# Token shift, masks, norm rows and value heads in other and wider operations, in a decoder layer of three mixers

## The chip, the cores and the metric

The kernel runs on one core of a Trainium2 chip. The metric is the device time of one execution in microseconds (us); less is better. A core has engines that each work through their own list of instructions in order: PE (TensorE, matrix multiplications; PEld is its loading of weights), DVE (VectorE), ACT (ScalarE), POOL (GpSimd) and SP (which here issues the DMA transfers). They wait for each other by semaphores.

## The reference, cut to what matters

One decoder layer for 512 tokens of width 1024: a norm, one input projection, three mixers side by side (NSA attention, RWKV-7, MoBA attention), an output projection, a ConvGLU and a last norm, all in float32. The change touches RWKV-7's input and its gating matrices, and NSA's values:

```python
def _rwkv7_mixer(p, mu, w0, w2, a0, a2, g2, k_k, k_a, r_k, lnx_w, lnx_b):
    p_prev = jnp.pad(p, ((0, 0), (1, 0), (0, 0)))[:, :-1]
    p = p + (p_prev - p) * mu                       # token shift
    r, k, v, xw, xa, xg = _split(p, [D_RWKV] * 3 + [32, 32, 64])
    w = jnp.exp(-RW_DECAY_SCALE * jax.nn.sigmoid((w0 + jnp.tanh(xw) @ w2).astype(f32)))
    a = jax.nn.sigmoid(a0 + xa @ a2)
    kk = heads(k * k_k)
    kk = kk / jnp.maximum(jnp.sqrt(jnp.sum(kk * kk, axis=-1, keepdims=True)), 1e-12)
    ...
def step(state, inp):                               # scanned over the 512 tokens
    r_t, w_t, k_t, v_t, kk_t, a_t = inp
    sa = jnp.einsum('bhvk,bhk->bhv', state, -kk_t)
    state = state * w_t[:, :, None, :] + sa[..., None] * (kk_t * a_t)[:, :, None, :] + v_t[..., None] * k_t[:, :, None, :]
    return state, jnp.einsum('bhvk,bhk->bhv', state, r_t)
```

NSA multiplies its probabilities with two pairs of value heads of 64 columns (`vs`, `vw`), which are columns of the input projection times the token's norm factor.

## The kernel before, in words

Features stand on the 128 partitions and tokens along the free axis, 512 at a time. A float32 product is made of three matmuls on operands split in a high and a low part (`mm3`, L238 to L243; `whi`, `wlo`, `xh`, `xl` are such parts); the high part is an ACT cast, the low part a DVE subtraction (L211, L213).

First four projections run side by side: the inputs of the decay and gate matrices (LORA) and `r`, `k`, `v` of the first RWKV head pair. After them `merge()` (L1030) interleaves generators: a stream of the other projections in the order of a list (`ks r1 v1 k1 nv q0 ...`), the two RWKV head pairs (`rw_run`, which calls `rw_pair`), and the attentions as their inputs come. Each `yield` carries a cost, and the generator with the least sum goes on. A scheduler of the framework then sets each engine's final list from that program order and its own estimate of when operands are ready, and gives each matmul result one of eight PSUM banks. So an edit that alters a few operations can reorder others and give banks to other results. From about 360 us on only the ConvGLU runs.

The parts that the change touches:

- `rw_in` (L319 to L337), once per RWKV input tile, seven tiles in all (four at the end of the first projections, then `r`, `v`, `k` of the second pair): `ex` is the projection times the norm factor (L325), `d` the difference of neighbour tokens (L330, and L331 for the first token), `rwin` = `d`·mu + `ex` (L335). The first tile is then put through tanh and sigmoid by ACT (L1062, L1063).
- `rw_pair` (L341), once per head pair: three matmuls on the LORA tile (L349, L353, L360); `ksq`, the square of `k`, by ACT (L374); its sums per head by PE (L379); a maximum by DVE (L383); a power by POOL (L386); `rnb`, four broadcast copies by DVE, each followed by a matmul that turns it (L394, L395); and `kkn`, the normalised key, which reads that PSUM bank (L398). Then products of chunks of 64 tokens (L450), masked into `GA` and `GR` (L456).
- The masks `NM` (L467) and `R` (L480), four operations of 128x128 each; `NM` reduced to `Nc` (L474) goes through DRAM to `NB` (L476, L478). A chain of 30 dependent DVE operations inverts 16x16 blocks (`X`, L488 to L490), a copy ends it (L492), and the result goes through DRAM again (L497, L499) to `DvT` and `Dv` (L502).
- `proj_v` (L717): per token tile 24 matmuls of 274 columns, then gates by ACT (L739), and for each of four heads an ACT operation for the high part (L742) and a DVE operation for the low part (L743).
- `evac_q` (L688), for a query tile: `P` (L690) takes it from PSUM, `qt` are its split parts (L695 by ACT, L696 by DVE), and `soft` (L769) starts with the matmul that reads `qt` (L779).

Of the kernel before, what the change touches and what calls it, by code (L numbers as in the profile page):

```python
# [36 lines left out]
F32 = mybir.dt.float32  # L37
F32R = mybir.dt.float32r
# [54 lines left out]
def hybrid_layer(ctx: ExitStack, tc: tile.TileContext, xT, cst, cols, lora, fgain, wA, wVn, cw1,  # L93
# [7 lines left out]
    def at(site):  # L101
        return pool if ENG[site] == 'p' else dve
# [21 lines left out]
    def r2(name, shape=(128, 512), dt=F32):  # L124
        return sb.tile(list(shape), dt, name=name, bufs=cap(name))
# [76 lines left out]
    omka = fixe(2)  # L202
    rcol = fixe(4)
# [108 lines left out]
    def consts_late():  # L312
        sp.dma_start(cstt, cst)
        sp.dma_start(lorat, lora)
        pool.tensor_copy(ident, ident0)
        dve.tensor_scalar(omka, colt[:, COLS["k_a"][0]:COLS["k_a"][0] + 2], -1.0, 1.0, op0=OP.mult, op1=OP.add)


    def rw_in(todo):  # L319

        mark('rwin')
        exs, ds, os_ = [], [], []
        for i, p in todo:
            ex = r2("ex")
            dve.tensor_tensor(ex, p, rstd_box[0], op=OP.mult)  # L325
            done()
            exs.append(ex)
        for ex in exs:
            d = r2("d")
            at('d').tensor_tensor(d[:, 1:512], ex[:, 0:511], ex[:, 1:512], op=OP.subtract)  # L330
            at('d').tensor_scalar(d[:, 0:1], ex[:, 0:1], -1.0, None, op0=OP.mult)  # L331
            ds.append(d)
        for (i, p), ex, d in zip(todo, exs, ds):
            o = r2("rwin")
            dve.scalar_tensor_tensor(o, d, col("mu", i), ex, op0=OP.mult, op1=OP.add)  # L335
            os_.append(o)
        return os_  # L337
# [3 lines left out]
    def rw_pair(p, r, k, v, L):  # L341
# [93 lines left out]
        bsel2 = bs_[:, None, :, None].to_broadcast([128, 2, 4, 16])  # L435
# [43 lines left out]
        for cc in range(4):  # L479
            dve.tensor_tensor(TS(R)[:, cc], GA[cc // 2][:, cc % 2, :, 0, :], con("offmask")[:, None, :].to_broadcast([128, 2, CH]), op=OP.mult)  # L480
# [236 lines left out]
    def proj_v():  # L717
# [835 lines left out]
```

## Time and profile before

| | |
|---|---|
| time, three runs | 729.62, 730.01, 731.35 us (median 730.01) |
| time of the profiled execution | 732.95 us |
| its span, first to last instruction | 731.1 us (so 1.85 us lie around it) |
| mean granted TensorE clock | 0.987 |
| busy | PE 701.1 us (96%), PEld 611.9, DVE 635.6 (87%), ACT 412.5 (56%), POOL 56.4 |

The profile is one execution recorded on the chip. A busy time counts the stretches in which an engine had an instruction under way; a wait is idle time before an instruction, put down to what released it. DVE's rows overlap a little: an instruction of 0.68 us starts 0.60 us after the one before it. The granted clock is a share of TensorE's full 2.4 GHz; 0.52 is about its lower level of 1.2 GHz.

### The profile page before, as it was taken

What the parts mean: (1) busy time and instruction counts of PE and PEld (TensorE: products, weight loads), DVE (VectorE), ACT (ScalarE), POOL (GpSimd) and SP (SyncE); (2) the same over time, 40 slices, a digit from 0 to 9 for tenths busy, and PEclk for the clock granted to TensorE, in tenths of its full rate; (3) what the DMA queues carried; (4) which work ended last, traced back from release to release, by engine and by line L of the source; (5) the groups of instructions that cost most, each with busy time, mean ns of one, the idle gap of its engine ahead of it and who ended that gap; (6) DMA issues with size and microseconds to landing.
All of it is one profiled execution on the core that took longest, in us unless ns stands there. A gap on an engine that the chain in (4) does not pass through costs nothing.

```text
span 731.1 us, 13614 instructions
## 1 busy us (share of the span) xinstructions
PE 701.1 (96%) x5146; PEld 611.9 (84%) x5146; DVE 635.6 (87%) x1394; ACT 412.5 (56%) x863; POOL 56.4 (8%) x71
## 2 busy tenths in 40 slices
PE   6999998899999999999989999999999999999995
PEld 4866977677788788877779999999999999998885
DVE  6589889768897999787999999999999999999804
ACT  7364544465656877863767546455464545657503
POOL 3110003000000010123320000000000000000001
PEclk9999999999999999999999999999999999999998
DMA  9613122513110013033308432323233333345003
GB/s 321 199 29 102 52 48 63 145 52 110 45 44 30 14 45 102 1 101 117 101 0 280 152 103 99 118 87 101 94 110 96 107 102 108 95 130 186 17 1 115
DMA packets 44658, 69.87 MB, mean 96 GB/s; under 512 B 10544, under 2 KB 12208, under 8 KB 44592
## 3 DMA queue, kind: packets, MB, share of 16 engines
q1 hardware_dynamic: 44016, 67.96, 29.4%
q8 instruction: 40, 0.66, 0.4%
q10 hardware_dynamic: 576, 1.05, 0.4%
q14 instruction: 26, 0.21, 0.1%
HBM read 64.40 MB, written 4.59 MB: 94 GB/s over the span
## 4 chain that ended last, share of the span: by engine, by line
PE 75%; DVE 13%; issue 4%; ACT 2%; DMA 2%; POOL 2%; SPq 0%; POOLq 0%; DVEq 0%; ACTq 0%
PE mm L241 6%; PE mm L243 6%; PE mm L242 6%; PE acc L242 5%; PE acc L241 5%; PE acc L243 5%; PE pB L241 3%; PE pB L243 3%; PE pC L241 3%; PE pB L242 3%; PE pC L242 3%; PE pC L243 3%; PE pA L241 3%; PE pA L243 3%; PE pA L242 3%
## 5 line engine op out<-in xcount | busy, mean ns | idle before, releaser
L1302 ACT CAST ah<-S 128x512 fp32r<-128x512 f32 x88 | 54.5, 621 | 60.8 <-DVE S L1297 60.6
L241 PE MATMUL mm<-xh,whi 128*128 128x512 f32 x152 | 68.3, 450 | 1.2 <-DVE Sall L622 1.2
L242 PE MATMUL acc<-dn,dn 128*128 128x512 f32 (+1 forms) x173 | 64.2, 371 | 0.0
L243 PE MATMUL acc<-dn,dn 128*128 128x512 f32 (+1 forms) x173 | 63.7, 370 | 0.0
L243 PE MATMUL mm<-xh,wlo 128*128 128x512 f32 x152 | 61.4, 404 | 0.0
L242 PE MATMUL mm<-xl,whi 128*128 128x512 f32 x152 | 61.1, 402 | 0.0
L1303 DVE TENSOR_TENSOR al<-S,ah 128x512 fp32r<-128x512 f32 x88 | 58.5, 682 | 0.8 <-ACT ah L1302 0.8
L211 ACT CAST whi<-wraw 128x512 fp32r<-128x512 f32 x70 | 42.4, 617 | 26.7 <-PE mm L242 11.9
L786 ACT ACTIVATE prob<-prob,fixed 128x128 f32<-128x128 f32 (+1 forms) x72 | 40.5, 564 | 26.9 <-DVE fixed L783 26.6
L241 PE MATMUL acc<-dn,dn 128*128 128x512 f32 (+1 forms) x173 | 55.7, 371 | 0.0
L241 PE MATMUL pB<-bh,ah 128*128 128x256 f32 x172 | 49.8, 290 | 0.0
L213 DVE TENSOR_TENSOR wlo<-wraw,whi 128x512 fp32r<-128x512 f32 x64 | 46.6, 734 | 2.9 <-PE mm L243 2.8
L241 PE MATMUL pC<-bh,ah 128*128 128x256 f32 x172 | 48.5, 282 | 0.2 <-ACT ah L1302 0.2
L243 PE MATMUL pB<-bh,al 128*128 128x256 f32 x172 | 48.6, 282 | 0.0
L243 PE MATMUL pC<-bh,al 128*128 128x256 f32 x172 | 48.5, 282 | 0.0
L242 PE MATMUL pC<-bl,ah 128*128 128x256 f32 x172 | 48.4, 281 | 0.0
L242 PE MATMUL pB<-bl,ah 128*128 128x256 f32 x172 | 48.3, 281 | 0.0
L1303 DVE TENSOR_TENSOR al<-wraw,ah 128x512 fp32r<-128x512 f32 x66 | 43.4, 681 | 0.0
L783 DVE CUSTOM_DVE_ANT_0 prob<-s,early 128x128 f32<-128x128 f32 (+1 forms) x72 | 34.6, 483 | 7.1 <-PE s L780 4.9
L818 ACT CAST ph<-pt 128x512 fp32r<-128x512 f32 (+3 forms) x72 | 29.4, 423 | 19.1 <-PE pt L811 18.3
L1302 ACT CAST ah<-wraw 128x512 fp32r<-128x512 f32 x66 | 36.7, 616 | 0.6 <-DMA wraw<-in_wF_dram 0.6
L242 PEld LDWEIGHTS acc<-dn,dn 128*128 128x128 f32 x173 | 32.7, 189 | 5.1 <-DVE dn L1366 0.2
(396 smaller groups left out, 2241.2 us busy)
## 6 DMA issues: line engine op xcount, KB each, us to landing
wraw<-in_wF_dram SPq DMA_DIRECT2D x88, 256.0 KB, 2.7
wraw<-in_wG_dram SPq DMA_DIRECT2D x44, 256.0 KB, 2.9
wraw<-in_wA_dram SPq DMA_DIRECT2D x38, 256.0 KB, 2.9
xr<-in_xT_dram SPq DMA_DIRECT2D x16, 256.0 KB, 4.9
wraw<-in_cw_dram SPq DMA_DIRECT2D x16, 256.0 KB, 3.2
wraw<-in_wO_dram SPq DMA_DIRECT2D x16, 256.0 KB, 2.6
fraw<-in_wA_dram SPq DMA_DIRECT2D x8, 256.0 KB, 5.6
x2d<-x2o SPq DMA_DIRECT2D x8, 256.0 KB, 3.7
```

Source lines behind the costliest of these rows:

```text
L211: act.copy(hi[:, :w], raw)
L213: (dve if dve_lo and (wcnt[0] % PLO or wcnt[0] < PLO0) else pool).tensor_tensor(lo[:, :w], raw, hi[:, :w].bitcast(F32), op=OP.subtract)
L241: pe.matmul(o, ah, bh, start=first, stop=False)
L242: pe.matmul(o, ah, bl, start=False, stop=False)
L243: pe.matmul(o, al, bh, start=False, stop=last)
L783: dve.tensor_tensor_reduce(out=P, in0=s_[:, 0:n], in1=con("cmask")[:, 512 - n:512], scale=1.0, scalar=3e38, op0=OP.add, op1=OP.min, accum_ ...
L786: act.activation(P, P, AF.Exp, bias=m, scale=-1.0, accum_out=sums[:, i, par:par + 1])
L818: act.copy(h, t_[:, 0:n])
L1302: act.copy(h, src)
L1303: at(f'L{i}').tensor_tensor(l, src, h.bitcast(F32), op=OP.subtract)
```

## The change

Token shift: `d` is gone. ACT writes `rwin` = `ex`·(1 − mu), and one DVE operation adds mu times the token before to columns 1 to 511. The column 1 − mu (`omu`) is made once. `rnb`: one copy of 128x512 for four of 128x128. `NM` and `R`: two operations of 128x256 each for four of 128x128. Value heads: one ACT and one DVE operation of 4x64 columns per token tile for four of each; they go into one tile `vn` for all heads, where there was a tile `vv` per head. A buffer less for `vv`. Beside that only two tables of sizes and the line of `omu` differ:

```diff
 
     def rw_in(todo):
 
         mark('rwin')
-        exs, ds, os_ = [], [], []
+        exs, os_ = [], []
         for i, p in todo:
             ex = r2("ex")
             dve.tensor_tensor(ex, p, rstd_box[0], op=OP.mult)
             done()
             exs.append(ex)
-        for ex in exs:
-            d = r2("d")
-            at('d').tensor_tensor(d[:, 1:512], ex[:, 0:511], ex[:, 1:512], op=OP.subtract)
-            at('d').tensor_scalar(d[:, 0:1], ex[:, 0:1], -1.0, None, op0=OP.mult)
-            ds.append(d)
-        for (i, p), ex, d in zip(todo, exs, ds):
+        for (i, p), ex in zip(todo, exs):
             o = r2("rwin")
-            dve.scalar_tensor_tensor(o, d, col("mu", i), ex, op0=OP.mult, op1=OP.add)
+            act.activation(o, ex, AF.Identity, scale=omu[:, i:i + 1])
             os_.append(o)
+        for (i, p), ex, o in zip(todo, exs, os_):
+            dve.scalar_tensor_tensor(o[:, 1:512], ex[:, 0:511], col("mu", i), o[:, 1:512], op0=OP.mult, op1=OP.add)
         return os_
 
     lock = [0]
@@ -389,9 +388,9 @@
         yield from want()
         prn = rbank()
         rb4 = r2("rnb", (128, 4, 2, 64))
+        dve.tensor_copy(rb4.rearrange("p a b c -> p (a b) c"), b3(rn2, 64))
         for t in range(NT):
             rb = rb4[:, t]
-            dve.tensor_copy(rb, b3(rn2[:, 2 * t:2 * t + 2], 64))
             pe.matmul(prn[:, t * 128:(t + 1) * 128], rb.rearrange("p a b -> p (a b)"), ident, start=True, stop=True)
         yield crw
         kkn = r2("kkn")
@@ -432,7 +431,6 @@
 
         R64 = ((0, 64), (64, 128))
         bs_ = con("bsel")
-        bsel2 = bs_[:, None, :, None].to_broadcast([128, 2, 4, 16])
         bsel4 = bs_[:, None, :, None].to_broadcast([128, 4, 4, 16])
         TS = lambda t: t.rearrange("p (c h x) -> p c h x", c=4, h=2)
 
@@ -463,9 +461,9 @@
         yield crw
         R, NM = r2("R"), r2("NM")
         NMv = NM.rearrange("p (c b j) -> p c b j", b=4, j=16)
-        for cc in range(4):
-            at('NM').tensor_tensor(NMv[:, 2 * cc:2 * cc + 2], GA[cc // 2][:, cc % 2, :, 0, :].rearrange("p h (b j) -> p h b j", b=4),
-                               bsel2, op=OP.mult)
+        for u in range(2):
+            at('NM').tensor_tensor(NMv[:, 4 * u:4 * u + 4], GA[u][:, :, :, 0, :].rearrange("p k h (b j) -> p (k h) b j", b=4),
+                               bsel4, op=OP.mult)
 
         XT, BT, st_, NX = (r2(n_) for n_ in ("X", "NB", "stmp", "Nc"))
         v16 = lambda z, u: z[0:64, u * 256:u * 256 + 256].rearrange("p (i j) -> p i j", j=16)
@@ -476,8 +474,9 @@
         sp.dma_start(s1.rearrange("c p j -> p c j"), Nc)
         NB = v16(BT, 0)
         sp.dma_start(NB, s1.rearrange("c (b i) j -> (c b) i j", b=8))
-        for cc in range(4):
-            dve.tensor_tensor(TS(R)[:, cc], GA[cc // 2][:, cc % 2, :, 0, :], con("offmask")[:, None, :].to_broadcast([128, 2, CH]), op=OP.mult)
+        for u in range(2):
+            dve.tensor_tensor(ch(R)[:, 4 * u:4 * u + 4], GA[u][:, :, :, 0, :].rearrange("p k h t -> p (k h) t"),
+                              con("offmask")[:, None, :].to_broadcast([128, 4, CH]), op=OP.mult)
         yield crw
         X = v16(XT, 0)
         pool.memset(X, 0.0)
@@ -727,7 +726,7 @@
                 (at('vwl') if i else dve).tensor_tensor(lo, r_, hi.bitcast(F32), op=OP.subtract)
                 wt.append((hi, lo))
             yield CW
-        vv = [q2("vv", (128, NT, 2, 64), F32R) for _ in range(4)]
+        vv = q2("vn", (128, NT, 4, 2, 64), F32R)
         for t in range(NT):
             yield from want()
             p = bank("mm")
@@ -737,13 +736,12 @@
                 if k % 2:
                     yield CW
             act.activation(gates[:, t, :], p[:, 256:274], AF.Sigmoid, scale=rcol[:, t:t + 1])
-            for h in range(4):
-                src = p[:, h * 64:(h + 1) * 64]
-                act.activation(vv[h][:, t, 0, :], src, AF.Identity, scale=rcol[:, t:t + 1])
-                dve.scalar_tensor_tensor(vv[h][:, t, 1, :], src, rcol[:, t:t + 1], vv[h][:, t, 0, :].bitcast(F32),
-                                         op0=OP.mult, op1=OP.subtract)
+            src = p[:, 0:256].rearrange("p (h d) -> p h d", h=4)
+            act.activation(vv[:, t, :, 0, :], src, AF.Identity, scale=rcol[:, t:t + 1])
+            dve.scalar_tensor_tensor(vv[:, t, :, 1, :], src, rcol[:, t:t + 1], vv[:, t, :, 0, :].bitcast(F32),
+                                     op0=OP.mult, op1=OP.subtract)
             done()
-        vn.extend(vv)
+        vn.extend(vv[:, :, h] for h in range(4))
 
     def evac_v(p, dst, j):
         P = q2("P")
```

A line of the kernel before stands one line lower in the changed one up to L313, and one or two lines higher behind it. PE has 3863 instructions in both; DVE has 1298 instead of 1330, ACT 682 instead of 678. Up to the value projection the lists of PE, DVE and ACT are in another order; behind the evacuation `cP` (L878, at 108 us in the trace) all of them are the same. Four places:

DVE around the norm row of the first head pair; `kl` is a low part of a key tile of the attention, `AR` and `kb` are factors of the chunk products. Before:

```order
L394 COPY rnb<-fixed 128x128 x4
L325 TENSOR_TENSOR ex<-mm,early 128x512
L213 TENSOR_TENSOR wlo<-wraw,whi 128x512
L330 TENSOR_TENSOR d<-ex 128x511
L331 TENSOR_SCALAR d<-ex 128x1
L398 SCALAR_TENSOR_TENSOR kkn<-rwin,fixed,rw 128x512
L335 SCALAR_TENSOR_TENSOR rwin<-d,fixed,ex 128x512
```

and now:

```order
L391 COPY rnb<-fixed 128x512
L214 TENSOR_TENSOR wlo<-wraw,whi 128x512
L411 TENSOR_TENSOR AR<-rwin,E 128x256
L416 TENSOR_TENSOR kb<-k_480,Ei 128x512
L710 TENSOR_TENSOR kl<-P,kk 64x512
L418 COPY fixed<-E 128x8
L710 TENSOR_TENSOR kl<-P,kk 64x512
L422 SCALAR_TENSOR_TENSOR rb__539<-rwin,fixed,k_480 128x512
L397 SCALAR_TENSOR_TENSOR kkn<-rwin,fixed,rw 128x512
```

Between the copy and `kkn` there stood four operations of the projections; now there are seven others, of this head pair, of a weight and of a key tile.

PE at the same place. The `[waits ...]` name the engines whose semaphores a row waits for; L395, now L394, turns the norm row. Before:

```order
L241 MATMUL mm<-xh,whi 128x512 [waits DVE_49]
L242 MATMUL mm<-xl,whi 128x512
L243 MATMUL mm<-xh,wlo 128x512
L395 MATMUL rw<-fixed,rnb 128x128 [waits DVE_49] x4
L241 MATMUL mm<-xh,whi 128x512
L242 MATMUL mm<-xl,whi 128x512
L243 MATMUL mm<-xh,wlo 128x512
L241 MATMUL mm<-xh,whi 128x512
```

and now:

```order
L394 MATMUL rw<-fixed,rnb 128x128 [waits DVE_49,PE_49]
L394 MATMUL rw<-fixed,rnb 128x128 x3
L242 MATMUL mm<-xh,whi 128x512
L243 MATMUL mm<-xl,whi 128x512
L244 MATMUL mm<-xh,wlo 128x512
L242 MATMUL mm<-xh,whi 128x512
L243 MATMUL mm<-xl,whi 128x512
L244 MATMUL mm<-xh,wlo 128x512
L242 MATMUL mm<-xh,whi 128x512 [waits DVE_49]
L243 MATMUL mm<-xl,whi 128x512
L244 MATMUL mm<-xh,wlo 128x512
```

The waiting row of the projection now follows six matmuls behind the turned rows, and what it waits for is `kkn`: the projection's result has been given the bank that `kkn` reads. Before, the row that waits in this piece stood ahead of the turned rows, and waited for an `ex`. The sums of `ksq` (L379, now L378) stand ten matmuls earlier in PE's list. SP's load of `NB` (L478) waited for the sums of the second pair; now it waits for the transfer to DRAM alone.

PE at the LORA matmuls of the second head pair. Before:

```order
L241 MATMUL mm<-xh,whi 128x512
L242 MATMUL mm<-xl,whi 128x512
L243 MATMUL mm<-xh,wlo 128x512
L349 MATMUL rw<-rwin,early 128x512
L353 MATMUL rw<-rwin,early 128x512
L360 MATMUL rw<-rwin,early 128x512 [waits DVE_49]
L241 MATMUL mm<-vw,xh 128x274
```

and now:

```order
L243 MATMUL mm<-xl,whi 128x512
L244 MATMUL mm<-xh,wlo 128x512
L348 MATMUL rw<-rwin,early 128x512 [waits DVE_49,PE_49]
L352 MATMUL rw<-rwin,early 128x512
L359 MATMUL rw<-rwin,early 128x512
L242 MATMUL mm<-vw,xh 128x274
```

L360 waited for the last `ex`, whose bank it writes; L359 waits for nothing, and L348 waits for a `GR` mask and chunk products of the first pair.

DVE behind the inverse of the first pair. Before:

```order
L492 COPY X<-X 64x256
L690 SCALAR_TENSOR_TENSOR P<-mm,early 128x512
L213 TENSOR_TENSOR wlo<-wraw,whi 128x512
L430 TENSOR_TENSOR bv<-rw,rwin 128x512
L696 TENSOR_TENSOR qt<-P,qt 64x512
L502 TENSOR_TENSOR DvT<-Nc,early 128x256 x2
L502 TENSOR_TENSOR Dv<-Nc,early 128x256 x2
L696 TENSOR_TENSOR qt<-P,qt 64x512
```

and now:

```order
L491 COPY X<-X 64x256
L416 TENSOR_TENSOR kb<-k_853,Ei 128x512
L214 TENSOR_TENSOR wlo<-wraw,whi 128x512
L501 TENSOR_TENSOR DvT<-Nc,early 128x256 x2
L501 TENSOR_TENSOR Dv<-Nc,early 128x256 x2
L689 SCALAR_TENSOR_TENSOR P<-mm,early 128x512
L214 TENSOR_TENSOR wlo<-wraw,whi 128x512
L429 TENSOR_TENSOR bv<-rw,rwin 128x512
```

`DvT` and `Dv` stood between the two `qt`, behind `P`; now they stand ahead of `P`, with a `kb` and another `wlo`.

## Rows read from the trace of the kernel before

**Rows 1.** The page: busy time of each engine, and the chain that ended last.

```profile
PE 701.1 (96%) x5146; PEld 611.9 (84%) x5146; DVE 635.6 (87%) x1394; ACT 412.5 (56%) x863; POOL 56.4 (8%) x71
...
PE 75%; DVE 13%; issue 4%; ACT 2%; DMA 2%; POOL 2%; SPq 0%; POOLq 0%; DVEq 0%; ACTq 0%
```

**Rows 2.** Waits of PE from 33 to 146 us: total, times, longest.

```profile
PE rw L527 <- DVE Y L567: 2.2, 1, 2.2
...
PE rw L360 <- DVE ex L325: 0.8, 1, 0.8
PE rw L360 <- ACT rwin L1063: 0.8, 1, 0.8
...
PE s L779 <- DVE qt L696: 0.3, 1, 0.3
```

**Rows 3.** Busy time in stretches: PE, PEld, DVE, ACT, POOL; granted clock; DMA share, GB/s.

```profile
39.50:42.90 3.40, 2.59 (x8) 0.95 (x9) 2.54 (x6) 3.36 (x6) 0.00 (x0) 1.00 0.52 149
42.90:46.30 3.40, 3.40 (x10) 2.62 (x9) 3.40 (x7) 3.03 (x5) 0.00 (x0) 0.52 0.02 5
70.20:73.60 3.40, 3.40 (x17) 3.40 (x17) 3.40 (x7) 3.10 (x5) 0.00 (x0) 0.52 0.15 18
97.50:100.90 3.40, 3.40 (x54) 2.77 (x54) 3.22 (x10) 0.68 (x3) 0.00 (x0) 1.00 0.21 59
118.00:121.40 3.40, 2.97 (x28) 2.97 (x30) 3.37 (x7) 0.59 (x1) 1.73 (x2) 0.52 0.04 16
```

**Rows 4.** Timeline of PE, 47 to 70 us: start, duration, instruction, wait before it.

```profile
47.97 0.95 PE L379 MATMUL rw<-early,ksq 128*128 128x2 f32 x8
...
52.29 1.16 PE L395 MATMUL rw<-fixed,rnb 128*128 128x128 f32 x8
53.21 0.47 PE L241 MATMUL mm<-xh,whi 128*128 128x512 f32 x1
...
68.93 1.12 PE L360 MATMUL rw<-rwin,early 64*128 64x512 f32 x2 [0.82 <-DVE ex L325]
```

**Rows 5.** Timeline of DVE, 49 to 55 us.

```profile
49.85 0.17 DVE L383 TENSOR_SCALAR fixed<-rw 128x8 f32<-128x8 f32 x1
50.05 0.42 DVE L412 TENSOR_TENSOR AR<-rwin,E 128x256 f32<-128x256 f32 x1
52.01 0.63 DVE L394 COPY rnb<-fixed 128x128 f32<-128x128 f32 x4 [1.54 <-POOL fixed L386]
...
53.16 0.68 DVE L213 TENSOR_TENSOR wlo<-wraw,whi 128x512 fp32r<-128x512 f32 x1
53.76 0.68 DVE L330 TENSOR_TENSOR d<-ex 128x511 f32<-128x511 f32 x1
54.36 0.14 DVE L331 TENSOR_SCALAR d<-ex 128x1 f32<-128x1 f32 x1
54.43 0.73 DVE L398 SCALAR_TENSOR_TENSOR kkn<-rwin,fixed,rw 128x512 f32<-128x512 f32 x1
```

**Rows 6.** Timeline of DVE, 91 to 99 us.

```profile
91.45 0.37 DVE L492 COPY X<-X 64x256 f32<-64x256 f32 x1
94.40 0.69 DVE L690 SCALAR_TENSOR_TENSOR P<-mm,early 128x512 f32<-128x512 f32 x1 [2.57 <-PE mm L243]
...
96.32 0.68 DVE L696 TENSOR_TENSOR qt<-P,qt 64x512 fp32r<-64x512 f32 x1
97.05 0.76 DVE L502 TENSOR_TENSOR DvT<-Nc,early 128x256 f32<-128x256 f32 x2
97.92 0.76 DVE L502 TENSOR_TENSOR Dv<-Nc,early 128x256 f32<-128x256 f32 x2
```

**Rows 7.** Timeline of SP's DMA queue at 94 us.

```profile
94.69 1.01 SPq L499 DMA_DIRECT2D Nc<-s  x2
```

**Rows 8.** Value heads' DVE group by shape: busy us, mean ns, idle before.

```profile
L743 DVE SCALAR_TENSOR_TENSOR vv<-mm,early,vv 128x64 fp32r<-128x64 f32 x16 | 4.4, 274 | 0.0
```

**Rows 9.** Group of a scaled ACT copy, 128x512: ns min/median/max, first and last start.

```profile
L866 ACT ACTIVATE oh<-tk,fixed x6: 687/690/717, 270.9 to 348.8; 128x512 fp32r<-128x512 f32 x6
```

More of the change, by code (lines that the diff above doesn't have):

```diff
@@ L71 @@
 NFIX = NCOLS + 16 + 512 + 4 + 128 + 8 * NSM
-NEARLY = NCST + 256 + 512 + 512 + 8 + 72 + 384
-CAPS = {'fraw': 8, 'xh': 8, 'xl': 8, 'fwh': 8, 'fwl': 8, 'rwin': 5, 'wraw': 6, 'whi': 6, 'wlo': 5, 'g': 3, 'AR': 4, 'eC': 2, 'bv': 6, 'G': 9, 'vv': 7, 'TA': 5, 'MU': 4, 'vt': 6, 'qt': 7, 'kl': 10, 'kk': 9, 'prob': 10, 'bhl': 8, 'ob': 8, 'oh': 8, 'ol': 7, 'pct': 4, 'sqo': 2, 'c0': 2, 'ono': 3, 'x2': 8, 'x2t': 8, 'ssum': 4, 'w2h': 7, 'w2l': 7, 'OPt': 2, 'cen': 3, 'o': 5, 'csq': 2, 'rb_': 6, 'sg': 2, 'hg': 2, 'sq2': 4, 'NM': 5, 'y': 14, 'E': 5, 'ct': 3, 'k2': 3, 'cP': 3, 'QT': 4, 'kt': 3, 's2': 2, 'sq': 2, 'Nc': 3, 'W0': 2, 'ZT': 4, 'kkn': 3, 'Sall': 6, 'cs': 5, 'DvT': 2, 'a': 3, 'R': 2, 'ph0': 5, 'ph1': 6, 'ph2': 4, 'pl0': 5, 'pl1': 7, 'on': 5, 'ex': 2, 'bb': 3, 'ah': 10, 'al': 7, 'xs': 4, 'tab': 2, 'bh512': 12, 'bl512': 12, 'actf': 23, 'cu': 3, 'u2': 3, 'x2o': 6, 'GA': 5, 'GR': 5, 'vw': 4, 'bhl256': 4, 'dn0': 3, 'dn1': 2, 'dn2': 4, 'dn3': 2, 'dnt0': 5, 'dnt1': 5, 'dnt2': 5, 'dnt3': 5, 'pl3': 2, 'ph3': 3, 'otmp': 4, 's1': 3}
+NEARLY = NCST + 256 + 512 + 512 + 8 + 7 + 72 + 384
+CAPS = {'fraw': 8, 'xh': 8, 'xl': 8, 'fwh': 8, 'fwl': 8, 'rwin': 5, 'wraw': 6, 'whi': 6, 'wlo': 5, 'g': 3, 'AR': 4, 'eC': 2, 'bv': 6, 'G': 9, 'vv': 6, 'TA': 5, 'MU': 4, 'vt': 6, 'qt': 7, 'kl': 10, 'kk': 9, 'prob': 10, 'bhl': 8, 'ob': 8, 'oh': 8, 'ol': 7, 'pct': 4, 'sqo': 2, 'c0': 2, 'ono': 3, 'x2': 8, 'x2t': 8, 'ssum': 4, 'w2h': 7, 'w2l': 7, 'OPt': 2, 'cen': 3, 'o': 5, 'csq': 2, 'rb_': 6, 'sg': 2, 'hg': 2, 'sq2': 4, 'NM': 5, 'y': 14, 'E': 5, 'ct': 3, 'k2': 3, 'cP': 3, 'QT': 4, 'kt': 3, 's2': 2, 'sq': 2, 'Nc': 3, 'W0': 2, 'ZT': 4, 'kkn': 3, 'Sall': 6, 'cs': 5, 'DvT': 2, 'a': 3, 'R': 2, 'ph0': 5, 'ph1': 6, 'ph2': 4, 'pl0': 5, 'pl1': 7, 'on': 5, 'ex': 2, 'bb': 3, 'ah': 10, 'al': 7, 'xs': 4, 'tab': 2, 'bh512': 12, 'bl512': 12, 'actf': 23, 'cu': 3, 'u2': 3, 'x2o': 6, 'GA': 5, 'GR': 5, 'vw': 4, 'bhl256': 4, 'dn0': 3, 'dn1': 2, 'dn2': 4, 'dn3': 2, 'dnt0': 5, 'dnt1': 5, 'dnt2': 5, 'dnt3': 5, 'pl3': 2, 'ph3': 3, 'otmp': 4, 's1': 3}
 PCAPS = {'mm': 7, 'rs': 5, 'rb': 4, 'rw': 6, 's': 7, 'pt': 4, 'ot': 7, 'tk': 2, 'ph': 7, 'ct': 2, 'vt': 2, 'oc': 4, 'acc': 8, 'g': 3, 'xt': 3, 'pA': 3, 'pB': 2, 'p': 2}
@@ L202, in hybrid_layer @@
     omka = fixe(2)
+    omu = fixe(7)
     rcol = fixe(4)
@@ L315, in consts_late @@
         pool.tensor_copy(ident, ident0)
+        dve.tensor_scalar(omu, colt[:, COLS["mu"][0]:COLS["mu"][0] + 7], -1.0, 1.0, op0=OP.mult, op1=OP.add)
         dve.tensor_scalar(omka, colt[:, COLS["k_a"][0]:COLS["k_a"][0] + 2], -1.0, 1.0, op0=OP.mult, op1=OP.add)
```

## The prediction

> **What bounds the kernel now.** I read the page first: PE is busy for 701.1 us of the span, 96%, and holds 75% of the chain that ended last; DVE comes next with 87% and 13% of that chain [rows 1]. So a DVE operation saved is worth nothing by itself. It counts where PE waits for it, and a reordered list counts where PE gets a new wait. The second view was the list of PE's waits over the stretch in which the lists differ: there are only a few, of 0.3 to 2.2 us [rows 2], and the LORA matmuls of the first head pair wait twice for 0.8 us, of which one row stands. Third came the granted clock by stretches [rows 3]. The reader is to see that a wait has a second price. After the stretch with the two ACT waits (39.50, PE busy 2.59 of 3.40) the next one is granted 0.52; after the wait of 0.82 before L360 [rows 4] the one from 70.20 is granted 0.52; after the wait of 2.2 for Y the one from 118.00 too. After the wait of 0.3 for qt the stretch from 97.50 kept 1.00. A stretch of 3.40 us at 0.52 does what 3.40 x 0.52 = 1.77 us do at full clock, so each costs 1.63 us. Last came the timelines at the places where the lists of PE or DVE have moved.
>
> **The change, place by place.** The sum is made against the profiled execution, 732.95 us: 731.1 of span and 1.85 around it. That execution stands 2.94 above the median of 730.01, so what I get is lowered by 2.94 at the end.
>
> Token shift, first four tiles. Per tile DVE loses two operations that take 0.60 + 0.07 = 0.67 us of its list (steps from 53.76 to 54.43, [rows 5]), and ACT gains one; the nearest row for it, a scaled copy of the same shape, is 0.69 us [rows 9]. The first tile's way from ex to tanh so stays as long as it was. PE gets to its LORA matmuls two matmuls earlier by its list, DVE gets to the tile somewhat earlier too. I take 0 and keep -0.8 (one of the two waits goes) to +0.7 (ACT, busy for 3.36 of 3.40 us there [rows 3], hands over one operation later). The half clock behind it stays.
>
> Norm row of the first pair. This is the new wait: the first matmul of the next projection needs the bank that kkn reads. Before, rnb came 52.01 - 47.97 = 4.04 us after the sums of ksq (L379) began [rows 4, 5]; of this 49.85 - 48.92 = 0.93 were DVE's backlog before the maximum, so 3.1 to 4.04. Behind the start of the copy DVE now has the copy itself (at most 0.55, from four that took 0.63), then wlo 0.60, AR 0.33, kb 0.60, kl 0.60, a small copy 0.08, kl 0.60, rb_ 0.66, then kkn 0.73 (shapes of [rows 5, 6], steps a little under the durations): 4.75 us. So kkn ends 7.8 to 8.8 us after the sums begin. PE has behind the sums (0.80) some 15 matmuls of 0.23, the four turned rows (53.21 - 52.29 = 0.92 [rows 4]) and six more matmuls: 0.80 + 3.45 + 0.92 + 1.4 = 6.6, and 7.0 if two of them still run at half clock. The wait is 0.8 to 1.8 us; if kkn's predecessors come early it can be 0, and below nothing is excluded, since PE did not wait there before. I take 1.0: the sums themselves stand ten matmuls earlier in PE's list and so will wait for ksq, which leaves DVE less backlog. Queued behind the waiting matmul is all of PE.
>
> The Trainium skill (Perfetto Trace Analysis, Optimizing Scalar/DVE Operations) speaks against the wide operations here: where ACT or DVE are not saturated but make another engine wait, splitting their instructions lets work finish sooner. The rows agree with it so far as the four copies of before let the first turned row start after a quarter of them; by this rule the single copy would add the 0.4 us between a quarter and the whole, a part of the 1.0 if PE is there by then.
>
> LORA matmuls of the second pair. L360 waited 0.82 us for ex and the stretch behind it ran at 0.52 [rows 3, 4]. Now no row of that kind waits: -0.82, and -1.63 for the clock, since PE is then busy through. Bounds: 0 (another wait takes its place, for the last tile now goes through ACT as well) to -2.45. I take -2.45: PE's list names no later partner there. PE is then 2.45 - 1.0 = 1.45 us ahead of before, until it needs the first query tile.
>
> The first query tile. DvT and Dv now stand ahead of P on DVE, and they wait for two DMA round trips behind the inverse. Before, P began at 94.40, when PE had finished the tile, and DVE had been idle for 2.57 us [rows 6]; DvT began 97.05 - 91.45 = 5.60 us after the copy X began, 2.36 us after SP issued the second transfer [rows 7], so nothing but the transfers sets it; DvT and Dv take another 1.6. P therefore starts 7.2 us after the copy, at 98.6 - x where x is what the copy gains, against 94.40: 4.2 - x later. For x: the value heads had 16 operations of 0.27 us, 0.20 in the list [rows 8]; four wide ones of some 0.33 (a 128x256 operation takes 0.42, [rows 5]) save 1.9. kb and wlo, now behind the copy, give 1.2. That is 3.1. Three token shifts (2.0), masks and norm rows (0.5, estimated from the same steps) could add 2.5, but a part of these falls before waits of DVE such as the 1.54 before rnb, where it is lost. I take 3.9, with 2.5 to 5.6 as ends. P and with it the matmul on qt come 0.3 later than before, although PE arrives 1.45 earlier: it waits 0.35 + 1.45 + 0.3 = 2.1 us. The lead is lost, and the wait is as long as that for Y, so I add one stretch at half clock, 1.63.
>
> Masks, value heads on PE's side. A token tile's PSUM bank is left sooner; PE did not wait for it [rows 2]. 0. If the cover, 24 matmuls per token tile, were gone, it would be 0.3 each. From cP on all lists are the same, so later waits shift along.
>
> Sum: 0 + 1.0 - 2.45 + 1.45 + 0.3 + 1.63 = +1.9; 732.95 + 1.9 - 2.94 = 731.9 us.
>
> **Rivals.** (a) Same waits, but the half clock does not follow the wait for qt, because the small matmuls around it keep PE at it: only +0.3, 730.3. For it: the stretch from 97.50 stayed at 1.00 last time; against it: that wait was 0.3, not 2.1.
>
> (b) The inverse gains all of 5.6: P then waits for PE again, 4.2 - 5.6 = -1.4, and the lead of 1.45 is kept, with no half clock behind it: 728.6; and 727.6 if the copy gains 1.0 more and nothing waits for kkn. For it: DVE had no idle time before any value head operation [rows 8], so it was full; and SP's load of NB, at the start of the inverse, no longer waits for L379. Against: its own waits further up.
>
> (c) Slower: the inverse is bound by its own length, 30 dependent operations and the transfers in front of it, and not by what DVE does between them. The saved value-head operations then leave holes, x falls to 2.5 or lower, P comes 1.7 later, with the half clock 3.3: 733.3. It decides from x below 2.9 on, where the sum passes +2.2 with some clock loss. For it: the wide operations save DVE time where it is interleaved with the chain; the second norm row still waits for POOL. Against: the idle time before those operations was 0.0 [rows 8].
>
> That the change does not do what it says is ruled out by the lists: 32 DVE rows fewer and four ACT rows more are there.
>
> **How the numbers follow.** Forecast 0.40, (a) 0.20, (b) 0.15, (c) 0.25. 0.3% of the time, about what a measurement of this kernel can tell from no change, is 2.2 us: faster is below 727.8, slower above 732.2. Of (b) a good half ends below 727.8 once small gains at the first tiles are added, and little of anything else: 0.11. Above 732.2 lie nearly all of (c) and some 0.13 of the forecast's 0.40, if x or the wait for kkn is at its end: 0.36. The rest, 0.53, is within. The range reaches from 728.0, in the middle of (b), to 734.2, (c) with x at 1.6. The forecast's own range is 730.8 to 733.0.
>
> **What would show it.** In the profile of the changed kernel: a wait of about 1 us of an mm matmul L242 for kkn L397 near 53 us; no wait before L359 near 68 us, and full clock in the stretch behind it; the copy L491 near 87.5 us; P L689 released by DVE's own list and not by PE; a wait of about 2 us of L777 for qt L695, and a stretch near 0.5 behind it; from cP on the same distances as before. The prediction is wrong if the copy gains under 2.5 or over 5.0 us, if the stretch behind 70 us is still at half clock, or if PE's waits before 108 us add up to the same while the time moves by more than 1 us.

## The result, and the profile after

The changed kernel takes 735.43 us (median of 6 runs, 734.81 to 738.71) where the kernel before takes 730.1 (6 runs, 729.58 to 731.55): a ratio of 1.0065, 95% interval 1.0046 to 1.0084. (The ratios here are the recorded ones; they differ a little from the quotient of the two medians, which is 1.0073 here.) A second set, with 12 executions of the changed kernel and 34 of the kernel before, gave 735.02 against 732.22, 1.0042 (1.0020 to 1.0064). The changed kernel is slower by 3 to 5 us. The forecast was 731.9 with a range of 728.0 to 734.2.

The profiled execution took 734.91 us with a span of 733.1. The page answers to [rows 1]:

```profile
PE 700.7 (96%) x5146; PEld 611.2 (83%) x5146; DVE 630.7 (86%) x1355; ACT 414.7 (57%) x858; POOL 56.7 (8%) x71
...
PE 74%; DVE 14%; DMA 4%; issue 3%; ACT 3%; POOL 2%; SPq 0%; POOLq 0%; ACTq 0%; DVEq 0%
```

DVE has lost 4.9 us of busy time and PE 0.4, and the share of DMA in the chain has gone from 2% to 4%. The list of PE's waits, 33 to 160 us (total, times, longest), answers to [rows 2]:

```profile
PE s L777 <- DVE qt L695: 3.0, 2, 2.5
PE rw L526 <- DVE Y L566: 2.2, 1, 2.2
PE mm L242 <- DVE kkn L397: 1.3, 1, 1.3
...
PE rw L359 <- ACT rwin L1061: 0.6, 1, 0.6
```

The wait for the last ex is gone, and there are the two new ones that the lists had shown: kkn, 1.3 us, and the first of the two for qt, 2.5. The first pair's LORA matmuls wait once for 0.6 us, not twice for 0.8. The places on PE's timeline (start, duration, instruction, wait before it); the second row answers to L360 of [rows 4] and has no wait, and the third is the first matmul of the `ks` projection, from which distances are taken below:

```profile
53.59 0.50 PE L242 MATMUL mm<-xh,whi 128*128 128x512 f32 x1 [1.33 <-DVE kkn L397]
```

```profile
69.16 1.12 PE L359 MATMUL rw<-rwin,early 64*128 64x512 f32 x2
```

```profile
34.68 0.48 PE L242 MATMUL mm<-xh,whi 128*128 128x512 f32 x1
...
98.00 0.33 PE L777 MATMUL s<-kk,qt 128*128 128x128 f32 x1 [2.46 <-DVE qt L695]
```

DVE around the norm row, answering to [rows 5]:

```profile
48.77 0.43 DVE L391 COPY rnb<-fixed 128x512 f32<-128x512 f32 x1 [1.54 <-POOL fixed L385]
...
52.13 0.75 DVE L422 SCALAR_TENSOR_TENSOR rb__539<-rwin,fixed,k 128x512 f32<-128x512 f32 x1
52.80 0.74 DVE L397 SCALAR_TENSOR_TENSOR kkn<-rwin,fixed,rw 128x512 f32<-128x512 f32 x1
```

kkn starts 4.0 us behind the start of the copy, where before it was 2.4. DVE behind the inverse, answering to [rows 6]:

```profile
88.21 0.39 DVE L491 COPY X<-X 64x256 f32<-64x256 f32 x1
...
94.00 0.76 DVE L501 TENSOR_TENSOR DvT<-Nc,early 128x256 f32<-128x256 f32 x2 [4.21 <-DMA Nc<-s]
94.68 0.75 DVE L501 TENSOR_TENSOR Dv<-Nc,early 128x256 f32<-128x256 f32 x2
95.35 0.68 DVE L689 SCALAR_TENSOR_TENSOR P<-mm,early 128x512 f32<-128x512 f32 x1
...
97.27 1.41 DVE L695 TENSOR_TENSOR qt<-P,qt 64x512 fp32r<-64x512 f32 x2
```

The copy comes 3.2 us earlier by the clock of the trace, then DVE stands idle for 4.21 us until the transfer lands, with P behind it although PE is past P's matmuls and, from 95.5 us on, waits for qt. Before, DVE was idle for 2.57 us and PE released P.

The granted clock (columns as in [rows 3]):

```profile
39.50:42.90 3.40, 2.82 (x9) 1.25 (x6) 2.01 (x4) 3.36 (x7) 0.00 (x0) 0.87 0.42 131
42.90:46.30 3.40, 3.40 (x16) 2.81 (x14) 2.76 (x5) 3.37 (x5) 0.00 (x0) 0.63 0.06 23
70.40:73.80 3.40, 3.40 (x28) 3.40 (x28) 3.40 (x5) 3.37 (x6) 0.00 (x0) 1.00 0.45 81
98.50:101.90 3.40, 3.40 (x55) 2.77 (x54) 2.99 (x11) 1.17 (x5) 0.00 (x0) 1.00 0.06 24
```

The stretch behind the second pair's LORA matmuls runs at full clock, as forecast. The one behind the wait for qt does too, against the forecast. Behind the first pair's LORA matmuls the half clock is still there in this execution (42.0 to 45.4 us). The value heads' operation, answering to [rows 8], and the new ACT operation of the token shift, answering to [rows 9]:

```profile
L741 DVE SCALAR_TENSOR_TENSOR vn<-mm,early,vn 128x256 fp32r<-128x256 f32 x4 | 1.9, 469 | 0.0
```

```profile
L332 ACT ACTIVATE rwin<-ex,early x7: 708/717/725, 36.3 to 70.5; 128x512 f32<-128x512 f32 x7
```

### The profile page after: what moved, and what is told of

It is laid out like the page before. It is cut to its first block, busy times and chain, and to the rows that moved or that the text cites. A ratio compares the mean times of both kernels' runs of the same rounds, so it can differ in the third digit from the quotient of the medians.

```text
span 733.1 us, 13567 instructions
## 1 busy us (share of the span) xinstructions
PE 700.7 (96%) x5146; PEld 611.2 (83%) x5146; DVE 630.7 (86%) x1355; ACT 414.7 (57%) x858; POOL 56.7 (8%) x71
## 4 chain that ended last, share of the span: by engine, by line
PE 74%; DVE 14%; DMA 4%; issue 3%; ACT 3%; POOL 2%; SPq 0%; POOLq 0%; ACTq 0%; DVEq 0%
PE mm L242 6%; PE acc L242 5%; PE acc L243 5%; PE mm L244 5%; PE acc L244 5%; PE mm L243 5%; PE pB L242 3%; PE pB L244 3%; PE pB L243 3%; PE pC L242 3%; PE pC L243 3%; PE pA L243 3%; PE pC L244 3%; PE pA L244 3%; PE pA L242 3%
## 5 line engine op out<-in xcount | busy, mean ns | idle before, releaser
L212 ACT CAST whi<-wraw 128x512 fp32r<-128x512 f32 x70 | 42.4, 618 | 21.3 <-PE mm L243 13.9
L242 PEld LDWEIGHTS mm<-xh,whi 128*128 128x128 f32 x152 | 28.9, 190 | 9.6 <-issue 2.1
```

What stands on the lines that cost most here:

```text
L212: act.copy(hi[:, :w], raw)
L242: pe.matmul(o, ah, bh, start=first, stop=False)
```

## The experiments

The first ks matmul begins anywhere between 32.3 and 34.8 us in these traces, so places are compared by their distance from that matmul. "To qt" is the distance to the first matmul on qt, "to cP" the one to the evacuation from which on the lists are the same. The sets of experiments ran on four chips; kernels of different sets are compared by their ratio to the kernel before, which ran in each set.

**The two kernels again.** No edit.

> The kernel before, unchanged, against itself: how far its profile varies from run to run. Theory A (the profiled execution of before, 2.9 us above its median, held half-clock stretches that most of its runs do not have, so that taking 2.94 off at the end was the failed step): runs near 730, the fast ones with a mean granted clock of about 0.990 to 0.992 against 0.987, and in the profile at least one of the four half-clock stretches (behind 43, 70, 118 and 142 us) gone or shorter. Theory B (the 2.94 us lie elsewhere, as in the transfers at the start or the end): clock 0.987 in the runs at 730 as well, the same four stretches, and another stretch shorter.

> The changed kernel, unchanged, a second profile. Both theories: 735 to 736 and a ratio of 1.006 to 1.008; PE waits of about 1.3 us for kkn at 53 us and about 2.5 us for qt at 98 us in every profile, since the lists set them. Theory A also expects its clock to vary by about the same as that of before.

Before against itself: 732.48 against 732.22, ratio 1.0011 (0.9992 to 1.0029), single executions from 730.1 to 737.5. After: 1.0042. In the second profile of before the stretches behind 70 and 118 us are at full clock and those behind 43 and 142 are not (here each is 6.8 us long), although the waits ahead of them are the same but for a few tenths; in the second of after none is low between 33 and 360 us. So a wait of the same length is followed by half clock in some executions and not in others: for Y PE waits 2.15 us in the first profile, with half clock behind it, and 2.17 in the second, without it. Which execution is which, these two did not settle: both profiles of before (732.95 and 736.05) lay above the median.

**DvT and Dv on POOL, in the changed kernel.**

```diff
-        for src, dst, eng in ((XX, DvT, dve), (X, Dv, at('dv'))):
+        for src, dst, eng in ((XX, DvT, pool), (X, Dv, pool)):
```

> The changed kernel with DvT and Dv formed by POOL instead of DVE; nothing else moves in DVE's, PE's or ACT's lists. Theory 1 (what costs is that P and qt stand behind DvT and Dv on DVE): the wait of the matmul on qt falls from 2.5 to below 0.7 us, PE keeps some 1.5 us, the time falls by 1.5 to 3 us to 732 to 734. Theory 2 (PE would wait at the next DVE result anyway, so the wait only moves): the wait for qt goes, another of over 1 us comes before 110 us, and the time stays within 0.7 us of 735.4.

729.23 us, ratio 0.9955 (0.9937 to 0.9974): 5.8 less than the changed kernel in the same set, about twice the most that theory 1 expected. The wait for qt is 0.7 us and PE releases P again:

```profile
86.13 0.38 DVE L491 COPY X<-X 64x256 f32<-64x256 f32 x1
...
91.14 0.69 DVE L689 SCALAR_TENSOR_TENSOR P<-mm,early 128x512 f32<-128x512 f32 x1 [3.43 <-PE mm L244]
...
93.06 2.08 DVE L695 TENSOR_TENSOR qt<-P,qt 64x512 fp32r<-64x512 f32 x2
```

**Four copies of rnb, in the changed kernel.**

```diff
-        dve.tensor_copy(rb4.rearrange("p a b c -> p (a b) c"), b3(rn2, 64))
         for t in range(NT):
             rb = rb4[:, t]
+            dve.tensor_copy(rb, b3(rn2[:, 2 * t:2 * t + 2], 64))
```

> The changed kernel with the four copies of rnb put back (the other three parts stay); with them the wait of the projection's matmul for kkn leaves PE's list, since that matmul gets another bank. Theory 1 (the wait for qt sets where PE stands at 98 us, and what PE loses before it is covered): the wait for kkn of 1.3 us is gone, the wait for qt grows by about as much, and the time stays within 0.7 us of 735.4. Theory 2 (the two waits add up): the time falls by 1 to 1.5 us to about 734.

733.58 us, ratio 1.0014 (0.9994 to 1.0035), 1.4 less than the changed kernel by the medians; but the executions overlap widely (732.9 to 737.9 against 732.1 to 739.3), so the times alone don't decide it. The trace does. The wait for kkn is gone, the one for qt is still 2.55, and the matmul on qt comes 60.9 us after the first ks matmul instead of 63.3, 62.6 and 63.1. Theory 1 falls: the wait for kkn is not covered by the later one, because it also holds up the products and masks that the inverse needs. The first chunk products come 25.8 us after the first ks matmul where they came 28.2, 27.5 and 27.4 us after it, and the copy behind the inverse 51.1 where it was 53.5, 53.0 and 53.1. What theory 2 says of the places holds; its 1 to 1.5 us of time are not shown.

**The kernel before with DvT and Dv on POOL.** The same edit as above on the kernel before.

> The kernel before with DvT and Dv formed by POOL. It tells what of the gain of the same edit in the changed kernel (5.8 us) belongs to the change's own order. Theory 1 (about half of it is the first pair's order, which the kernel before does not have, the rest is the second pair's wait for Sall at 140 us, which both have): ratio 0.995 to 0.998 against before, 728.5 to 730.5 where before is 732.2; in the profile the wait for Sall or DvT near 140 us goes, the one for qt at 97 us hardly changes. Theory 2 (all of it is the change's own cost): 0.999 to 1.001.

734.19 against 731.52 us, ratio 1.0028 (1.0008 to 1.0048). Both theories fall: the edit costs 2 to 3 us here. The wait for qt at the first pair stays 0.35, since P and qt were ahead already. At the second pair the wait for Sall goes, but DvT on POOL is waited for, and so is the next query tile:

```profile
139.09 1.25 PE L527 MATMUL rw<-DvT,R 64*64 64x64 f32 x32 [0.78 <-POOL DvT L502]
...
143.40 0.33 PE L779 MATMUL s<-kk,qt 128*128 128x128 f32 x1 [1.71 <-DVE qt L696]
```

These waits add up to 2.5 us, where PE waits 1.9 to 2.4 us at the same place in the four profiles of the kernel before, so they don't account for the whole cost; the rest is open. But the gain on the changed kernel is not a gain of the edit as such.

**The parts by themselves.** The token shift alone on the kernel before, and the changed kernel without it:

```diff
-            d = r2("d")
-            at('d').tensor_tensor(d[:, 1:512], ex[:, 0:511], ex[:, 1:512], op=OP.subtract)
-            at('d').tensor_scalar(d[:, 0:1], ex[:, 0:1], -1.0, None, op0=OP.mult)
...
+            act.activation(o, ex, AF.Identity, scale=omu[:, i:i + 1])
...
+            dve.scalar_tensor_tensor(o[:, 1:512], ex[:, 0:511], col("mu", i), o[:, 1:512], op0=OP.mult, op1=OP.add)
```

> The token shift alone on the kernel before. Its lists have DvT and Dv ahead of P, as in the changed kernel, and two value-head operations behind the copy too; no matmul waits for kkn, and none of the second pair's LORA matmuls waits for ex. Theory 1 (the waits of the lists make the time, and a half-clock stretch behind a wait comes in some executions only): a wait of 2 to 4 us for qt, ratio 1.000 to 1.004. Theory 2 (the shift's gain at the second pair's LORA matmuls, 0.8 and a half-clock stretch of 1.6, counts in each run): ratio 0.996 to 0.999.

> The changed kernel with the old token shift: norm row, masks and value heads in wide operations. Its lists have P ahead of DvT and Dv, and both qt behind them; the wait for ex stays at 68 us, none for kkn. Theory 1 (place of DvT and Dv against P and qt decides): a wait for qt of 1 to 3 us in place of 0.35, ratio 1.001 to 1.005. Theory 2 (the cost of the change is the token shift through ACT): ratio 0.998 to 1.001.

735.65 us, ratio 1.0046 (1.0024 to 1.0068), with a wait for qt of 2.0; and 734.74 us, ratio 1.0047 (1.0027 to 1.0067), with one of 2.2. Each half of the change costs about as much as the whole, so the costs are not those of the parts' operations: both put the transfers' landing ahead of qt, once with P behind DvT and Dv, once with P ahead and both qt behind. The half without the shift was split once more:

> The value heads' wide operations alone on the kernel before. DVE's list has P, DvT and Dv, then both qt, so that qt waits for the transfers. Theory 1: a wait for qt of 1 to 3 us instead of 0.35, ratio 1.001 to 1.005. Theory 2 (the slower part without the token shift came from the norm row or the masks): ratio 0.998 to 1.001, and a wait for qt under 1 us.

> Norm row and masks alone on the kernel before; PE's list as before but for four rows, P and the first qt ahead of DvT. Theory 1: the waits of before, ratio 0.998 to 1.001. Theory 2 (the single copy of rnb makes PE wait): a wait of over 1 us for rnb and ratio 1.001 to 1.004.

Value heads alone: 735.09 us, ratio 1.0034 (1.0011 to 1.0057). Norm row and masks alone: 732.41, ratio 1.0001 (0.9983 to 1.0019), and a wait for qt of 0.35. Here DVE with the value heads alone:

```profile
91.93 0.69 DVE L690 SCALAR_TENSOR_TENSOR P<-mm,early 128x512 f32<-128x512 f32 x1 [2.77 <-PE mm L243]
94.02 0.76 DVE L502 TENSOR_TENSOR DvT<-Nc,early 128x256 f32<-128x256 f32 x2 [1.40 <-DMA Nc<-s]
...
96.14 1.41 DVE L696 TENSOR_TENSOR qt<-P,qt 64x512 fp32r<-64x512 f32 x2
```

P is there at 91.93, as PE releases it, and qt starts 4.2 us later instead of 1.9 [rows 6], behind DvT and Dv. With norm row and masks alone PE waits 1.0 us for the single copy of rnb, but so it does for the four copies of the kernel before in an execution without half clock ahead of them (the one at 729.35 us, below). From the lists of PE's waits, the single copy first:

```profile
PE rw L395 <- DVE rnb L392: 1.0, 1, 1.0
```

```profile
PE rw L395 <- DVE rnb L394: 1.0, 1, 1.0
```

The Trainium skill (Perfetto Trace Analysis, Optimizing Scalar/DVE Operations) says that breaking up instructions may let work finish sooner, where ACT or DVE are not saturated but leave other engines idle. These two rows show nothing gained by four copies over one.

**Four copies of rnb, and DvT and Dv on POOL.** Both edits on the changed kernel.

> The changed kernel with four copies of rnb and with DvT and Dv on POOL: neither the wait for kkn nor DvT and Dv ahead of P. Theory 1 (the waits for kkn and for qt are the change's whole cost and add up): 1 to 2 us faster than with POOL alone (729.2), 727 to 728.5, ratio 0.993 to 0.995. Theory 2 (what is saved at kkn is lost at the next wait): as with POOL alone, 0.9955.

728.22 against 731.52 us, ratio 0.9949 (0.9929 to 0.9970), the fastest of all kernels; with POOL alone it was 0.9955, too near to tell apart by the times. The trace tells it: to qt 59.8 us instead of 61.2.

**More executions of both kernels.**

> The kernel before, one more profiled execution. Theory A (most executions of before run near 730 because they lack the half-clock stretches behind 43 and 70 us, which both profiles so far had, and the changed kernel's waits of 2.5 us for qt and 1.3 for kkn come in all of its executions): an execution near 730 has at most one stretch below 0.97 between 38 and 75 us, and its matmul on qt comes at most 61.5 us after the first ks matmul, against 63.3 and 62.7 in the two slower profiles. Theory B (where PE stands at the matmul on qt does not tell the executions apart; the 3 us lie behind 108 us): the distance is 62.7 to 63.3 in an execution near 730 as well.

> The same kernel and the same theories as the run before it: one more execution, so that at least one of them is likely to be near 730. Theory A: each stretch at half clock between 38 and 75 us that an execution lacks brings the matmul on qt 1 to 1.7 us nearer to the first ks matmul. Theory B: no such relation.

> The changed kernel, a third profiled execution. Theory A: the distance from the first ks matmul to the one on qt lies within 62.4 to 63.4 us whatever the clock did before it, since P stands behind DvT, Dv and the transfers, and PE waits 2 to 2.6 us there. Theory B: the distance varies with the clock as in the kernel before.

They took 733.32, 729.35 and 735.97 us. The one of before at 729.35, stretches and the two places:

```profile
39.50:42.90 3.40, 2.59 (x9) 1.34 (x8) 2.54 (x6) 3.36 (x7) 0.00 (x0) 1.00 0.51 154
42.90:46.30 3.40, 2.99 (x14) 2.16 (x12) 3.40 (x8) 3.04 (x5) 0.00 (x0) 1.00 0.00 0
70.20:73.60 3.40, 3.40 (x30) 3.40 (x28) 3.40 (x7) 3.08 (x5) 0.00 (x0) 1.00 0.19 24
```

```profile
33.63 0.48 PE L241 MATMUL mm<-xh,whi 128*128 128x512 f32 x1
```

```profile
94.84 0.33 PE L779 MATMUL s<-kk,qt 128*128 128x128 f32 x1 [0.35 <-DVE qt L696]
```

No stretch is low, and to qt it is 61.21 us; in the other one, equally clean (without half clock up to there), 61.19. In the two earlier profiles it was 63.30 (97.06 less 33.76, rows below) and 62.67, each with a loss of clock between 38 and 75 us that sums to 3.4 us by the stretches' shares; in the second of them all of it lies behind 43 us.

```profile
33.76 0.48 PE L241 MATMUL mm<-xh,whi 128*128 128x512 f32 x1
...
97.06 0.33 PE L779 MATMUL s<-kk,qt 128*128 128x128 f32 x1 [0.35 <-DVE qt L696]
```

Theory A holds for this place, with one thing beside the clock: the clean executions also wait less for ACT ahead of the first pair's LORA matmuls, 0.15 and 0.22 us instead of 0.80 and 0.50. The two rows are of the profile of before and of the execution at 729.35:

```profile
39.38 0.69 PE L349 MATMUL rw<-rwin,early 32*128 32x512 f32 x1 [0.80 <-ACT rwin L1062]
```

```profile
38.66 0.69 PE L349 MATMUL rw<-rwin,early 32*128 32x512 f32 x1 [0.22 <-ACT rwin L1062]
```

What makes that wait differ is not settled. Theory A does not hold for the whole time: the execution of 733.32 is as clean up to 108 us, and lost its 4 us behind that.

The changed kernel's third execution, its place and the stretches around it:

```profile
32.34 0.48 PE L242 MATMUL mm<-xh,whi 128*128 128x512 f32 x1
...
95.48 0.47 PE L777 MATMUL s<-kk,qt 128*128 128x128 f32 x1 [2.72 <-DVE qt L695]
```

```profile
92.10:95.50 3.40, 0.68 (x19) 0.44 (x11) 3.34 (x8) 1.92 (x3) 0.00 (x0) 0.98 0.17 57
95.50:98.90 3.40, 3.40 (x20) 2.66 (x21) 2.58 (x8) 1.10 (x3) 0.00 (x0) 0.50 0.17 53
98.90:102.30 3.40, 3.40 (x38) 2.82 (x37) 0.89 (x4) 0.60 (x2) 0.00 (x0) 0.52 0.00 0
```

To qt it is 63.1 us, as forecast by theory A (the wait of 2.7 us is a little over the 2 to 2.6 named), and this time two stretches at half clock follow the wait: to cP it is 77.1 us, against 74.3 and 73.5 in the other two profiles of it and 72.2 in the clean ones of before. From qt to cP that is 13.9 us instead of 11.0. The profiles with the value heads alone (to cP 77.7) and with four rnb copies (74.8) show two such stretches behind the same wait too, and the one without the shift (75.9) shows one; the one with the shift alone shows none. None of the three profiles with DvT and Dv of the first pair on POOL in the changed lists has one there.

**The first pair alone on POOL, in the changed kernel.**

```diff
-        for src, dst, eng in ((XX, DvT, dve), (X, Dv, at('dv'))):
+        for src, dst, eng in ((XX, DvT, dve if p else pool), (X, Dv, dve if p else pool)):
```

> The changed kernel with DvT and Dv on POOL for the first head pair alone; only their four rows leave DVE's list. Theory 1 (the place of DvT and Dv ahead of P and qt is worth the 1.3 to 2.1 us that the matmul on qt is late against undisturbed executions of before): the matmul on qt comes 61.2 us after the first ks matmul again, the time falls by 1.3 to 2.5 us to 732.5 to 734, ratio 1.001 to 1.003. Theory 2 (the rest of the 5.8 us too comes from there, by later half-clock stretches that do not come): ratio 0.995 to 0.998.

731.34 against 731.91 us, ratio 0.9978 (0.9955 to 1.0002; 0.9992 by the medians), where the changed kernel had 1.0042 and 1.0065 in its own sets: 3.4 and 5.9 us by the differences of the medians, 4.7 and 6.4 by the ratios, for four rows that leave DVE's list. In the trace the lists of PE and ACT and the rest of DVE's are unchanged. That is more than the 1.3 to 2.5 us of theory 1; by the ratio it lies at the edge of theory 2's range, by the medians between the two. To qt it is 61.5 us, to cP 72.5, and the wait for qt is 0.6 (the profiled execution itself took 734.70 us, with half clock from 143.5 to 150.3 us):

```profile
87.64 0.38 DVE L491 COPY X<-X 64x256 f32<-64x256 f32 x1
...
92.65 0.69 DVE L689 SCALAR_TENSOR_TENSOR P<-mm,early 128x512 f32<-128x512 f32 x1 [3.43 <-PE mm L244]
...
94.58 1.98 DVE L695 TENSOR_TENSOR qt<-P,qt 64x512 fp32r<-64x512 f32 x2
```

## Why the prediction was wrong

- **First tiles of the token shift** (0 taken, -0.8 to +0.7): one wait of 0.6 instead of two of 0.8. The small gain is within the bounds. The ACT operation takes 0.717 us, near the 0.69 taken.
- **Norm row** (+1.0 taken, 0.8 to 1.8): 1.3 us, by the mechanism named, in all three profiles (1.3, 1.4, 1.3). Its price was right as a wait; that it also delays the inverse was missed, and the run with four copies of rnb shows it.
- **The inverse's gain** (x of 3.9, ends 2.5 and 5.6): by distance from the first ks matmul 4.2, 4.7 and 4.6 against the profile on which the sum was made. Against an undisturbed execution of before (copy at 89.95, 56.3 us after the first ks matmul) 2.8 to 3.4. Of its parts, the wide value-head operations take 0.47 us each and 0.40 in the list, where 0.33 was taken.
- **The first query tile**: PE waits 2.5, 2.3 and 2.7 us, 2.1 forecast; P is released by DVE's own list, as forecast. Rival (b) does not happen. Rival (c) with an x of 2.5 or less does not either. The 5.60 us from copy to DvT were luck as a price of the transfers: in [rows 6] DvT follows qt with no idle time (96.32 + 0.68 against 97.05), so it was the list that set it. Where DVE waits for the transfers, in the changed kernel, it is 5.8, 5.6 and 6.0.
- **LORA matmuls of the second pair** (-0.82 and -1.63): the wait is gone and the clock stays up. But the 1.63 was taken as a price that every execution of before pays, and three of the four profiles of before ran the stretch behind 70 us at full clock, with a wait for ex of 0.7 to 0.8 ahead of it. In the sum this does no harm: the 1.0 for kkn, the -2.45 here and the 1.45 that PE waits longer for qt cancel.
- **The half clock behind qt** (+1.63): in one profile of three, and there it costs 3.0 us from qt to cP.
- **The end of the sum** ("what I get is lowered by 2.94"): this is the step that failed. The sum in the profiled execution's own time was 734.85, and the changed kernel's profiled execution took 734.91. Part of that agreement is chance, since the trace of after starts its first ks matmul 0.9 us later. But taking off 2.94 supposes that the changed kernel's usual execution is faster than this by as much as that of before, and it is not. What is left in the sum at qt is +0.3, against a matmul on qt that in the profiled execution came 2.1 us later than in a clean one. In the changed kernel that matmul hangs on the copy, the transfers and DVE's list, and it came 62.6 to 63.3 us after the first ks matmul, with half clock before it or without. So a clean execution of before loses 1.3 to 2.1 us by the change up to there, and these could not be taken off. And 2.94 was itself too large for a usual execution: it is the distance to the median of three, 730.01, while the larger sets of the kernel before have medians of 732.2, 731.5 and 731.9 (34, 33 and 29 executions, each set on a chip of its own).

Made against a clean execution, the sum would have been: no clock to win back, and a matmul on qt that comes 62.6 to 63.3 us after the first ks matmul instead of 61.2, so +1.3 to +2.1, and half clock behind a wait of over 2 us in some executions (3.0 us where two stretches of it come). Taking the first pair's DvT and Dv out of DVE's list takes most of the delay and the half clock away in each of the three profiles without them, and 3 to 6 us of the time. Not settled is what makes up the rest of the 3 to 5 us. More half clock on the average of executions seems not to be it: in the second set the mean granted clock is 0.991 over the 34 executions of before and 0.991 over the 12 of the changed kernel, whose mean time is 3 us longer; among the 34, an execution with 0.001 less clock is 0.34 us slower (an estimate, by a straight line through them). From cP to the last matmul the distances are 614.0 to 618.0 us in four profiles of before and 616.1 to 617.0 in three of after, which overlap. All three profiles of after have a stretch near half clock between 372 and 379 us that none of the four of before has, with the same lists there; but the kernel before with DvT and Dv on POOL has it too, and the changed one with four rnb copies has not, so it does not belong to the change alone.

## What to carry to other kernels

A sum made against one profiled execution is made against that execution's clock. Before counting a half-clock stretch as something that a change wins back, or taking a slow execution's excess off the result, look at whether the same stretch is low in a second profile, and ask whether the place that the change moves would have been late without it; a median of three executions is a weak guide to what is usual. An instruction that waits for a DMA round trip holds all that stands behind it on its engine (here P, for which PE was done). So after any edit that moves a list, look for what now stands behind such an instruction; here four rows moved to an engine that is 8% busy made the difference between a ratio of 1.004 to 1.007 and one of 0.998. Fewer and wider operations on an engine that is not the bound gave nothing by themselves where that was tried (1.0001 for norm row and masks), and the value heads and the token shift, each by itself, cost time with waits for qt of 2.6 and 2.0 us that came with the reordering. Where the 0.5% comes from by which the changed kernel without its two waits is faster than the kernel before, is not taken apart by any run.

## What the runs showed of the hardware beside that

The same wait of TensorE is followed by half clock or not, from one execution of the same program to the next: PE waits 0.82 us for ex ahead of the second pair's LORA matmuls in the profile of before and in the execution at 729.35 us, and the stretch from 70.20 us, busy throughout in both, was granted 0.52 in the first [rows 3] and 1.00 in the second. The two stretches behind 40 us are no such pair: in the profile of before two waits of 0.8 lie ahead (the stretch from 39.50 holds only the second of them, the first ended at 39.38), in the other execution waits of 0.22 and 0.81.

And POOL, busy for 9% of the span in the changed kernel with DvT and Dv on POOL, forms DvT of the first pair in two operations of 0.6 us each and Dv in two of 1.0, against 0.42 each on DVE; spans on POOL are rough in these profiles:

```profile
92.39 1.18 POOL L501 TENSOR_TENSOR DvT<-Nc,early 128x256 f32<-128x256 f32 x2 [9.08 <-DMA Nc<-s]
93.53 2.08 POOL L501 TENSOR_TENSOR Dv<-Nc,early 128x256 f32<-128x256 f32 x2
```
